# An encoder block with 32 experts: each partition takes four adjacent weight rows, in a ring of ten slots of 2 MB

## The chip, the cores and the metric

The kernel runs on one core of one Trainium2 chip. The metric is the device time of one execution in microseconds. Before the change the median of three runs is 1483.31 us (1477.65 to 1484.72).

## What is computed

One layer of a streaming encoder on 256 tokens of width 1024, in float32: a mixer of stick-breaking attention and a state-space scan, cross-attention into 256 memory tokens, and a mixture of 32 experts of which each token takes four. Only the last part is touched:

```python
def expert(xt, e):            # xt: the rows of tokens that chose expert e
    g = min(xt @ w_e_gate[e] + b_e_gate[e], 7.0)
    u = clip(xt @ w_e_up[e] + b_e_up[e], -7.0, 7.0)
    return (g * sigmoid(1.702 * g) * (u + 1)) @ w_e_down[e] + b_e_down[e]
h = layer_norm(alpha * h + sum(weight[t, e] * expert(h[t], e) for the 4 experts of t))
```

Each of the three matrices of an expert is 1024 x 1024 float32, 4 MB; all 96 are read, 384 MB.

## The kernel before

Up to about 530 us the mixer and the attentions run; their weights (`W`) come through SP's DMA queue, are split by ScalarE and VectorE into two parts (L96, L97) and multiplied on TensorE (L241 to L244). From then on the experts run, in 8 quads of four, each quad in two pairs.

*Weights.* An expert's matrix is fetched in chunks (`fetch`, `slot`), in the order gate and up of one expert, gate and up of its neighbour, down of both. A chunk is 256 rows of 1024 numbers, 1 MB: partition p takes the two adjacent rows 2p and 2p + 1, 8 KB in one run. The ring has 21 slots of 8 KB per partition, in four pools (`MR = 7, 7, 3, 4`) that open as space comes free. SP issues a fetch into a slot once the matmuls that read it are done. While the attention runs, each load of its weights lets one fetch of the first pool follow (`W.beside`).

*Matmuls.* `matmul_cols` (L950) multiplies a chunk: for each of the two rows k and each half i of the 1024 columns one matmul of 64 slots (tokens) by 512 columns. The 64 tokens of an expert are gathered from the normalised rows by a one-hot matrix (`gather`, L979): the rows x are the operand that is loaded into the array, 128 of their columns at a time. As partition p of a chunk holds rows 2p and 2p + 1, the columns are taken at every second place: `pairs(kt)` is `slice(256 * (kt // 2) + kt % 2, 256 * (kt // 2) + 256, 2)`. The gathered block xg gets the gain and bias of the norm (`gb2`, laid out in the same way). Gate and up (with a bias matmul L904 first, by `bias`) go to PSUM banks; `swiglu` (VectorE L955, L957 to L959, ScalarE L956) makes `ut`; `act_t` (L967) transposes it with four matmuls, again with columns at every second place; the down matmuls (`ps_y`, L950) follow, and `scatter` (L1000 to L1002) adds the result to the rows.

There are 32 gather matmuls per quad (8 column tiles, two parts of x, two token blocks) and four transposes per expert.

*Order.* A recording layer sets the order on each engine from the operations and its own costs, mixing pieces of neighbouring experts; a bias matmul for the next expert needs a PSUM bank whose previous tenant VectorE has read. SP, TensorE, VectorE and ScalarE each take their rows in that order.

*Further blocks.* If an expert has more than 64 tokens, a loop under a branch (`overflow`, L1083) runs the rest after quad 3, with weights in slots of the ring that the surrounding fetches leave free (four slots). With these inputs the loop has no turn, but each engine passes the branch. The last expert's w_down is fetched in smaller pieces (256 KB, in column quarters) for a finer end.

Of the kernel before, what the change touches and what calls it, by code (L numbers as in the profile page):

```python
# [39 lines left out]
MR = 7, 7, 3, 4  # L40
# [78 lines left out]
def body(nc, tc, a, out, dbg=None, stop=99):  # L119
# [7 lines left out]
    with es:  # L127
# [505 lines left out]
        if stop <= 2:  # L633
# [8 lines left out]
                for c in range(4)]  # L642
# [3 lines left out]
        def slot():  # L646
            turn[0] += 1
            return ring[(turn[0] - 1) % nslots].tile([P, 2, D], F32, tag="mw", name="mw")

        def fetch(upto):  # L650

            if not looped[0]:
                upto = min(upto, len(plan) // 2 + nslots - 4)
            while len(got) < min(upto, len(plan)):
                w, e, c = plan[len(got)]
                t = slot()
                if w == 2 and e == NE - 1:

                    t = t.rearrange("p j (k i f) -> p (j k) i f", k=2, i=2)
                    v = wes[w][e].rearrange("(c g p k) (j i f) -> c g p k j i f", c=2, g=2, p=P, j=2,  # L660
                                            i=2)[c % 2, :, :, :, :, c // 2]
                    for g in range(2):
                        for i in range(2):
                            nc.sync.dma_start(t[:, 2 * g:2 * g + 2, i], v[g, :, :, i])
# [61 lines left out]
        rows2 = xt_p.tile([8, 256], F32, name="rows2")  # L726
        for j, n in enumerate(("ln2_g", "ln2_b")):
            nc.sync.dma_start(rows2[4 * j:4 * j + 4], a[n][0].rearrange("(c f) -> c f", f=256))
# [4 lines left out]
        nc.vector.tensor_copy(gb2, ps[:, :16].rearrange("p (k j) -> p k j", k=2))  # L733
# [212 lines left out]
        def matmul_cols(dst, lhs, chunk, c, first=False):  # L946

            for k in range(2):
                for i in range(2):
                    nc.tensor.matmul(dst[i], lhs(2 * c + k), chunk[:, k, 512 * i:512 * i + 512],  # L950
                                     start=first and c == 0 and k == 0, stop=c == 3 and k == 1,
                                     skip_group_check=True)
# [8 lines left out]
        def pairs(kt):  # L961

            return slice(256 * (kt // 2) + kt % 2, 256 * (kt // 2) + 256, 2)

        def act_t(ut, pa, aT):
            for f in range(4):
                nc.tensor.transpose(pa[:, P * f:P * f + P], ut[:, pairs(f)], ident)  # L967
            nc.scalar.activation(aT, pa.rearrange("p (f i c) -> p f i c", f=4, i=2), AF.Copy)  # L968

        def gather(sel, xg, n, ps, kts=(0, KT)):  # L970

            w = 512 // n
            for kt in range(*kts, w):
                p = ps()
                for i in range(w):
                    o = p[:, n * i:n * i + n]
                    for x in (xh, xl):
                        for b in range(NB):
                            nc.tensor.matmul(o, x[:, b, pairs(kt + i)], sel[:, b], start=i == 0 and b == 0 and x is xh,  # L979
                                             stop=b == NB - 1 and x is xl, skip_group_check=True)  # L980
                for i in range(w):
                    o, g, b_ = p[:, n * i:n * i + n], *[gb2[:, (kt + i) % 2, 4 * j + (kt + i) // 2:4 * j + (kt + i) // 2 + 1]
# [74 lines left out]
        def overflow():  # L1057

            nv = nc.values_load(nov[0:1, 0:1], min_val=0, max_val=15)
            wb = [slot() for _ in range(3)]  # L1060
            ys = slot().rearrange("p k (h f) -> p (k h) f", h=2)
            ys = [ys[:, k].bitcast(F32R) for k in range(4)]
# [20 lines left out]
            with tc.If(nv > 0), tc.For_i(0, nv, 1):  # L1083
# [27 lines left out]
                n = 0  # L1111
                dst = [[pg[0][0:64], pg[0][64:128]], [pg[1][0:64], pg[1][64:128]], [y2[0][0:64], y2[1][64:128]]]
                for w in range(3):
# [3 lines left out]
                    for c in range(4):  # L1117
                        wt = wb[n % 3]
                        n += 1
                        nc.sync.dma_start(wt, wes[w][bass.ds(ev, 1), 256 * c:256 * c + 256].rearrange(  # L1120
                            "o (p k) f -> p (o k) f", p=P))
# [239 lines left out]
```

## Time and profile before

| | |
|---|---|
| median of 3 runs | 1483.31 us |
| profiled execution, its own time | 1483.58 us |
| its span | 1481.9 us |
| TensorE busy | 1391.4 us, 94% |
| DMA | 489.69 MB, mean 330 GB/s |
| mean granted TensorE clock | 0.985 |

The page lists what each engine did in one profiled execution. PE is TensorE's matmuls, PEld its weight loads, which overlap with them; DVE is VectorE, ACT ScalarE, SP the engine that issues the DMAs (SPq its queue). A duration of a matmul in a row of its own is longer than the distance between two of them, since they overlap; the distance is read from a run: its length over its number. A wait is idle time of an engine, with what ended it.

### The profile page before, as it was taken

What the parts mean: (1) busy time and instruction counts of PE and PEld (TensorE: products, weight loads), DVE (VectorE), ACT (ScalarE), POOL (GpSimd) and SP (SyncE); (2) the same over time, 40 slices, a digit from 0 to 9 for tenths busy, and PEclk for the clock granted to TensorE, in tenths of its full rate; (3) what the DMA queues carried; (4) which work ended last, traced back from release to release, by engine and by line L of the source; (5) the groups of instructions that cost most, each with busy time, mean ns of one, the idle gap of its engine ahead of it and who ended that gap; (6) DMA issues with size and microseconds to landing.
All of it is one profiled execution on the core that took longest, in us unless ns stands there. A gap on an engine that the chain in (4) does not pass through costs nothing. (4 is left out here: it accounts for less than half of the span.)

```text
span 1481.9 us, 19128 instructions
## 1 busy us (share of the span) xinstructions
PE 1391.4 (94%) x7888; PEld 802.9 (54%) x7888; DVE 635.1 (43%) x1004; ACT 416.4 (28%) x656; POOL 16.8 (1%) x36
## 2 busy tenths in 40 slices
PE   7999998998999999999999999979999999998996
PEld 7989898997999853333333333324334333323332
DVE  7766568998886551532222121222212212222213
ACT  5575678886555410010010000001001001001010
POOL 1000000000000010000000000000000000000001
PEclk9999999999999999999999999999999999999998
DMA  7545345543685789999999999999999999999995
GB/s 244 171 163 179 124 162 171 199 153 132 254 298 177 284 316 421 420 393 413 418 420 420 419 420 420 419 419 373 419 419 420 420 419 420 419 419 419 420 420 202
DMA packets 103503, 489.69 MB, mean 330 GB/s; under 512 B 10422, under 2 KB 15030, under 8 KB 54774
## 3 DMA queue, kind: packets, MB, share of 16 engines
q1 hardware_dynamic: 103140, 488.17, 83.2%
q8 instruction: 63, 1.03, 0.3%
q10 hardware_dynamic: 274, 0.27, 0.1%
q14 instruction: 26, 0.21, 0.0%
HBM read 487.33 MB, written 1.08 MB: 330 GB/s over the span
## 5 line engine op out<-in xcount | busy, mean ns | idle before, releaser
L950 PE MATMUL ps_gu<-mw,xg 128*64 128x512 f32 x2048 | 464.0, 595 | 1.0 <-DMA mw<-in_w_e_up 1.0
L950 PEld LDWEIGHTS ps_gu<-mw,xg 128*64 128x64 f32 x2048 | 146.5, 137 | 271.3 <-issue 256.5
L950 PE MATMUL ps_y<-mw,aT 128*64 128x512 f32 x992 | 225.4, 597 | 1.7 <-DMA mw<-in_w_e_down 1.6
L97 DVE TENSOR_TENSOR w_l<-w_raw,w_h 128x1024 fp32r<-128x1024 f32 x145 | 175.3, 1215 | 87.4 <-ACT w_h L96 85.5
L96 ACT ACTIVATE w_h<-w_raw 128x1024 fp32r<-128x1024 f32 x145 | 152.8, 1056 | 117.2 <-PE ps_t L243 73.0
L241 PE MATMUL ps_t<-hTh,w_h 128*128 128x256 f32 x576 | 164.0, 286 | 2.0 <-DVE gx L331 2.0
L243 PE MATMUL ps_t<-hTl,w_h 128*128 128x256 f32 x576 | 164.1, 285 | 0.0
L244 PE MATMUL ps_t<-hTh,w_l 128*128 128x256 f32 x576 | 162.7, 284 | 0.3 <-DVE w_l L97 0.3
L950 PEld LDWEIGHTS ps_y<-mw,aT 128*64 128x64 f32 x992 | 71.8, 138 | 137.5 <-issue 130.6
L241 PEld LDWEIGHTS ps_t<-hTh,w_h 128*128 128x128 f32 x576 | 110.0, 191 | 3.3 <-issue 3.1
L957 DVE TENSOR_SCALAR ut<-ps_gu 128x512 f32<-128x512 f32 x32 | 22.1, 691 | 206.3 <-PE ps_gu L950 206.1
L243 PEld LDWEIGHTS ps_t<-hTl,w_h 128*128 128x128 f32 x576 | 110.1, 191 | 0.2 <-issue 0.2
L244 PEld LDWEIGHTS ps_t<-hTh,w_l 128*128 128x128 f32 x576 | 109.6, 191 | 0.5 <-DVE w_l L97 0.5
L968 ACT ACTIVATE aT<-ps_x 128x512 f32<-128x512 f32 x32 | 19.1, 597 | 314.0 <-PE ps_x L967 313.9
L904 PE MATMUL ps_gu<-bgu,ident 128*64 128x512 f32 x256 | 72.0, 630 | 28.9 <-DVE ut L957 13.5
L955 DVE TENSOR_SCALAR gt<-ps_gu 128x512 f32<-128x512 f32 x32 | 22.1, 690 | 158.4 <-PE ps_gu L950 158.4
L995 DVE SCALAR_TENSOR_TENSOR y<-ps_y,scl,y 128x512 fp32r<-128x512 f32 x30 | 22.5, 750 | 153.5 <-ACT y L994 147.7
L994 ACT ACTIVATE y<-ps_y,scl 128x512 fp32r<-128x512 f32 x30 | 19.0, 684 | 222.2 <-PE ps_y L950 177.7
L956 ACT ACTIVATE st<-gt 128x512 f32<-128x512 f32 x32 | 20.1, 629 | 198.2 <-DVE gt L955 198.2
L904 PEld LDWEIGHTS ps_gu<-bgu,ident 128*64 128x64 f32 x256 | 17.1, 141 | 73.2 <-DVE ut L957 29.5
L1002 DVE TENSOR_TENSOR h<-h,ps_x 128x512 f32<-128x512 f32 x60 | 38.7, 681 | 15.2 <-PE ps_x L1001 15.2
L987 ACT ACTIVATE xg<-ps_x,gb 128x256 f32<-128x256 f32 x32 | 18.1, 564 | 94.4 <-PE ps_x L979 94.4
(354 smaller groups left out, 1798.3 us busy)
## 6 DMA issues: line engine op xcount, KB each, us to landing
mw<-in_w_e_gate SPq DMA_DIRECT2D x128, 1024.0 KB, 19.9
mw<-in_w_e_up SPq DMA_DIRECT2D x128, 1024.0 KB, 10.2
mw<-in_w_e_down SPq DMA_DIRECT2D x124, 1024.0 KB, 19.9
w_raw<-in_w_in SPq DMA_DIRECT2D x39, 1024.0 KB, 5.4
w_raw<-in_w_ssd SPq DMA_DIRECT2D x8, 1024.0 KB, 5.0
w_raw<-in_w_sb SPq DMA_DIRECT2D x4, 1024.0 KB, 5.1
csb<-csd SPq DMA_DIRECT2D x8, 512.0 KB, 6.4
w_raw<-in_w_mix_out SPq DMA_DIRECT2D x4, 1024.0 KB, 5.1
```

The lines of the kernel that those rows point to most:

```text
L96: nc.scalar.activation(h, src, AF.Copy)
L97: nc.vector.tensor_tensor(l, src, h.bitcast(F32), op=ALU.subtract)
L241: nc.tensor.matmul(o, wh[:, k, s], xh[:, kt], start=first and j % 2 == 0, stop=False, skip_group_check=True)
L243: nc.tensor.matmul(o, wh[:, k, s], xl[:, kt], start=False, stop=False, skip_group_check=True)
L244: nc.tensor.matmul(o, wl[:, k, s], xh[:, kt], start=False, stop=last, skip_group_check=True)
L904: nc.tensor.matmul(pg[w][64 * i:64 * i + 64], hot4(2 * w + i), bgu, start=True, stop=False, skip_group_check=True)
L950: nc.tensor.matmul(dst[i], lhs(2 * c + k), chunk[:, k, 512 * i:512 * i + 512], start=first and c == 0 and k == 0, stop=c == 3 and k == 1, ...
L955: nc.vector.tensor_scalar(gt, pg[0], LIMIT, None, op0=ALU.min)
L956: nc.scalar.activation(st, gt, AF.Sigmoid, scale=1.702)
L957: nc.vector.tensor_scalar(ut, pg[1], -LIMIT, LIMIT, op0=ALU.max, op1=ALU.min)
L995: nc.vector.scalar_tensor_tensor(yl[r], y2[i][r], scl[r, i:i + 1], yh[r].bitcast(F32), op0=ALU.mult, op1=ALU.subtract)
L1002: nc.vector.tensor_tensor(h2[:, b, s], h2[:, b, s], ps, op=ALU.add)
```

## The change

A chunk becomes 512 rows, 2 MB: partition p takes the four adjacent rows 4p to 4p + 3, 16 KB in one run. The ring has ten slots of 16 KB per partition (`MR = 3, 3, 2, 2`). The columns of x and `ut` are therefore taken at every fourth place (`fours`), and gb2 is laid out to match, with four small transposes in place of two. Each chunk has eight matmuls. The loop for further blocks takes one slot and uses its halves in turn; its result's buffer (`o_ys`) and the last gains (`gb3`) have a pool of their own, `spare`. The last w_down is fetched in the same pieces of 256 KB, laid out for the new rows.

```diff
-MR = 7, 7, 3, 4
+MR = 3, 3, 2, 2
...
-                for c in range(4)]
+                for c in range(2)]
...
-            return ring[(turn[0] - 1) % nslots].tile([P, 2, D], F32, tag="mw", name="mw")
+            return ring[(turn[0] - 1) % nslots].tile([P, 4, D], F32, tag="mw", name="mw")
...
-                upto = min(upto, len(plan) // 2 + nslots - 4)
+                upto = min(upto, len(plan) // 2 + nslots - 1)
...
-                ins = nc.sync.dma_start(t, wes[w][e, 256 * c:256 * c + 256].rearrange("(p k) f -> p k f", p=P))
+                ins = nc.sync.dma_start(t, wes[w][e, 512 * c:512 * c + 512].rearrange("(p k) f -> p k f", p=P))
...
-        gb2 = cst.tile([P, 2, 8], F32, name="gb2")
+        gb2 = cst.tile([P, 4, 4], F32, name="gb2")
...
-        for k in range(2):
-            nc.tensor.transpose(ps[:, 8 * k:8 * k + 8], rows2[:, k:256:2], ident[:8, :8])
+        for k in range(4):
+            nc.tensor.transpose(ps[:, 4 * k:4 * k + 4], rows2[:, k:512:4], ident[:4, :4])
...
+        spare = es.enter_context(tc.tile_pool(name="spare", bufs=1, reuse_waits="tile"))
...
-            for k in range(2):
-                for i in range(2):
-                    nc.tensor.matmul(dst[i], lhs(2 * c + k), chunk[:, k, 512 * i:512 * i + 512],
+            for k in ks:
+                for i in range(2):
+                    nc.tensor.matmul(dst[i], lhs(4 * c + k), chunk[:, k, 512 * i:512 * i + 512],
...
-        def pairs(kt):
-            return slice(256 * (kt // 2) + kt % 2, 256 * (kt // 2) + 256, 2)
+        def fours(kt):
+            return slice(512 * (kt // 4) + kt % 4, 512 * (kt // 4) + 512, 4)
...
-                nc.tensor.transpose(pa[:, P * f:P * f + P], ut[:, pairs(f)], ident)
+                nc.tensor.transpose(pa[:, P * f:P * f + P], ut[:, fours(f)], ident)
...
-                            nc.tensor.matmul(o, x[:, b, pairs(kt + i)], sel[:, b], start=i == 0 and b == 0 and x is xh,
+                            nc.tensor.matmul(o, x[:, b, fours(kt + i)], sel[:, b], start=i == 0 and b == 0 and x is xh,
...
-            wb = [slot() for _ in range(3)]
-            ys = slot().rearrange("p k (h f) -> p (k h) f", h=2)
+            wb = slot()
+            ys = spare.tile([P, 4, 512], F32R, tag="spare", name="o_ys")
```

The added line moves the lines behind it by one: L950, L967, L979 and L1083 of before are L951, L968, L980 and L1084 after.

The order on TensorE is laid out anew. First, on TensorE in the second pair of a quad, where the up matmuls of an expert end (ps_gu_6769 before, ps_gu_6672 after), with the bias matmuls of the next tenant of that bank (ps_gu_7045 and ps_gu_6924) and the down matmuls (ps_y). Before:

```order
L950 MATMUL ps_gu_6769<-mw,xg 64x512 x16
L904 MATMUL ps_gu_7045<-bgu,ident 64x512 x2
L950 MATMUL ps_y_6690<-mw,aT 64x512
L950 MATMUL ps_y_6691<-mw,aT 64x512
L950 MATMUL ps_y_6690<-mw,aT 64x512
L950 MATMUL ps_y_6691<-mw,aT 64x512
L967 MATMUL ps_x<-ident,ut 128x128 x4
```

And after, at the same place:

```order
L951 MATMUL ps_gu_6672<-mw,xg 64x512 x16
L951 MATMUL ps_y_6601<-mw,aT 64x512
L951 MATMUL ps_y_6602<-mw,aT 64x512
L951 MATMUL ps_y_6601<-mw,aT 64x512
L951 MATMUL ps_y_6602<-mw,aT 64x512
L951 MATMUL ps_y_6601<-mw,aT 64x512
L951 MATMUL ps_y_6602<-mw,aT 64x512
L951 MATMUL ps_y_6601<-mw,aT 64x512
L951 MATMUL ps_y_6602<-mw,aT 64x512
L904 MATMUL ps_gu_6924<-bgu,ident 64x512 x2
L968 MATMUL ps_x<-ident,ut 128x128 x4
```

The two bias matmuls stood right behind the last matmul of the bank's previous tenant; now a chunk of eight down matmuls stands between.

Second, on SP around the branch of the loop (the loop's own DMAs left out, which stand between the two pieces of each). Before:

```order
L668 DMA mw<-in_w_e_down 128x2048
L1083 COMPARE_AND_BRANCH x2
...
L1083 UNCONDITIONAL_BRANCH x2
L668 DMA mw<-in_w_e_down 128x2048 x3
L668 DMA mw<-in_w_e_up 128x2048
```

And after:

```order
L668 DMA mw<-in_w_e_down 128x4096
L1084 COMPARE_AND_BRANCH x2
...
L1084 UNCONDITIONAL_BRANCH x2
L668 DMA mw<-in_w_e_gate 128x4096
L668 DMA mw<-in_w_e_down 128x4096 x3
L668 DMA mw<-in_w_e_gate 128x4096 x2
```

Before, the first fetches behind the branch finish the down matrix whose first chunk stands ahead of it; after, one gate chunk comes first.

## Rows read from the trace of the kernel before

**Rows 1.** The page's first two parts: the span; busy time, share and number of instructions of each engine; and the span in 40 equal slices of 37 us (busy tenths of TensorE and its granted clock; the DMA engines' share in tenths; GB/s), with the number of DMA packets and their bytes below.
```profile
span 1481.9 us, 19128 instructions
...
PE 1391.4 (94%) x7888; PEld 802.9 (54%) x7888; DVE 635.1 (43%) x1004; ACT 416.4 (28%) x656; POOL 16.8 (1%) x36
...
PE   7999998998999999999999999979999999998996
...
PEclk9999999999999999999999999999999999999998
DMA  7545345543685789999999999999999999999995
GB/s 244 171 163 179 124 162 171 199 153 132 254 298 177 284 316 421 420 393 413 418 420 420 419 420 420 419 419 373 419 419 420 420 419 420 419 419 419 420 420 202
DMA packets 103503, 489.69 MB, mean 330 GB/s; under 512 B 10422, under 2 KB 15030, under 8 KB 54774
```

**Rows 2.** Three windows of the expert stage: window and its length in us, busy time and instructions of each engine, granted clock, share of the DMA engines, GB/s.
```profile
core 0: us, PE busy (x) PEld busy (x) DVE busy (x) ACT busy (x) POOL busy (x), PEclk, DMA share, GB/s
...
640.00:1000.00 360.00, 333.82 (x1556) 124.45 (x1552) 83.27 (x144) 30.96 (x51) 0.00 (x0) 0.99 1.01 416
...
1061.00:1320.00 259.00, 244.54 (x1132) 90.65 (x1128) 60.06 (x103) 22.52 (x37) 0.00 (x0) 0.99 1.01 419
1320.00:1440.00 120.00, 109.87 (x522) 41.11 (x524) 26.74 (x46) 11.46 (x19) 0.00 (x0) 1.00 1.01 420
```

**Rows 3.** TensorE's waits: which matmul (tile and line) waited for which instruction; us in total, times, the longest. First between 640 and 1000 us, then the two for weights between 1061 and 1482 us.
```profile
PE ps_gu L904 <- DVE ut L957: 6.3, 8, 0.8
PE ps_x L1000 <- ACT y L994: 4.7, 6, 0.8
PE ps_gu L904 <- DVE gt L955: 4.0, 5, 0.8
PE ps_x L1000 <- DVE h L1002: 3.4, 4, 0.8
PE ps_x L967 <- DVE ut L959: 1.2, 2, 0.6
PE ps_x L979 <- DVE h L1002: 0.5, 2, 0.3
...
PE ps_y L950 <- DMA mw<-in_w_e_down: 1.6, 3, 0.6
PE ps_gu L950 <- DMA mw<-in_w_e_up: 1.0, 3, 0.6
```

**Rows 4.** The chain of waits between 1000 and 1062 us, in order of time: start, duration, engine, tile, line, and how many instructions in a run.
```profile
1006.69 2.12 PE ps_x L979 x16
...
1009.83 1.17 PE ps_x L979 x8
...
1028.82 1.72 PE ps_gu L950 x8
1030.53 0.68 PE ps_x L967 x4
```

**Rows 5.** Four lines by themselves (L967, L979, L858, L241): weight loads (PEld) or matmuls (PE), their number, shortest, median and longest duration in ns, first and last start, and shapes.
```profile
L967 PEld LDWEIGHTS ps_x<-ident,ut x128: 194/209/219, 562.9 to 1448.9; 128*128 128x128 f32 x128
L967 PE MATMUL ps_x<-ident,ut x128: 281/283/386, 562.9 to 1449.0; 128*128 128x128 f32 x128
...
L979 PEld LDWEIGHTS ps_x<-sel,xh x128: 192/198/333, 535.1 to 1356.0; 128*128 128x128 f32 x128
L979 PE MATMUL ps_x<-sel,xh x128: 280/284/583, 535.1 to 1356.1; 128*128 128x256 f32 x128
L979 PEld LDWEIGHTS ps_x<-sel,xl x128: 193/198/331, 535.5 to 1356.2; 128*128 128x128 f32 x128
...
L858 PE MATMUL ps_l<-wr,x2T x32: 192/276/297, 522.9 to 529.7; 128*128 128x32 f32 x32
...
L241 PEld LDWEIGHTS ps_t<-hTh,w_h x576: 186/188/337, 13.2 to 376.9; 128*128 128x128 f32 x192
```

**Rows 6.** TensorE's timeline around 528 us: start, duration of the run, line, output and operands, shapes, number.
```profile
528.02 1.97 PE L858 MATMUL ps_l<-wr,x2T 128*128 128x32 f32 x16 [0.25 <-ACT x2T L855]
```

**Rows 7.** Windows ahead of the expert stage, columns as in rows 2.
```profile
20.00:30.00 10.00, 10.00 (x88) 10.00 (x87) 5.26 (x8) 5.74 (x9) 0.00 (x0) 1.00 0.75 219
100.00:200.00 100.00, 100.00 (x733) 89.53 (x733) 62.82 (x78) 67.43 (x102) 0.00 (x0) 1.00 0.48 159
...
300.00:400.00 100.00, 94.06 (x748) 87.81 (x747) 86.76 (x113) 68.88 (x111) 1.56 (x5) 0.97 0.50 179
```

**Rows 8.** TensorE's waits for VectorE at the bias matmuls over the whole span, columns as in rows 3.
```profile
PE ps_gu L904 <- DVE ut L957: 13.5, 17, 0.8
...
PE ps_gu L904 <- DVE gt L955: 9.4, 12, 0.8
```

**Rows 9.** The longest wait of SP's queue (SPq), columns as in rows 3.
```profile
SPq L82 <- DVE w_l L97: 333.2, 58, 12.5
```

**Rows 10.** TensorE's timeline behind the branch; in brackets the idle time ahead and what ended it (PEq is TensorE's sequencer).
```profile
1000.21 6.48 PE L904 MATMUL ps_gu<-bgu,ident 128*64 128x512 f32 x16 [6.00 <-PEq L1083]
```

**Rows 11.** Two windows of 20 us behind the branch, columns as in rows 2.
```profile
1000.00:1020.00 20.00, 19.79 (x88) 8.71 (x89) 4.50 (x12) 2.26 (x4) 0.00 (x0) 0.85 0.90 372
1020.00:1040.00 20.00, 20.00 (x96) 8.08 (x95) 3.46 (x5) 1.86 (x3) 0.00 (x0) 1.00 0.93 378
```

More of the change, by code (lines that the diff above doesn't have):

```diff
@@ L945, in body, with matmul_cols @@
         ring += [p for p, n in zip((mr2, mr3, mr4), MR[1:]) for _ in range(n)]
-        def matmul_cols(dst, lhs, chunk, c, first=False):
-            for k in range(2):
+        def matmul_cols(dst, lhs, chunk, c, first=False, ks=range(4)):
+            for k in ks:
                 for i in range(2):
-                    nc.tensor.matmul(dst[i], lhs(2 * c + k), chunk[:, k, 512 * i:512 * i + 512],
-                                     start=first and c == 0 and k == 0, stop=c == 3 and k == 1,
+                    nc.tensor.matmul(dst[i], lhs(4 * c + k), chunk[:, k, 512 * i:512 * i + 512],
+                                     start=first and c == 0 and k == 0, stop=c == 1 and k == 3,
                                      skip_group_check=True)
@@ L1059, in overflow @@
             nv = nc.values_load(nov[0:1, 0:1], min_val=0, max_val=15)
-            wb = [slot() for _ in range(3)]
-            ys = slot().rearrange("p k (h f) -> p (k h) f", h=2)
-            ys = [ys[:, k].bitcast(F32R) for k in range(4)]
+            wb = slot()
+            ys = spare.tile([P, 4, 512], F32R, tag="spare", name="o_ys")
+            ys = [ys[:, k] for k in range(4)]
             sel = mt.tile([P, NB, 4, CAP], F32R, tag="sel", name="o_sel")
@@ L1116, in overflow @@
                         act_t(ut, pa, aT)
[L1117 to L1121, printed above, removed]
-                        lhs = (lambda kt: aT[:, kt % 4, kt // 4]) if w == 2 else (lambda kt: xg[:, kt, 0:CAP])
-                        matmul_cols(dst[w], lhs, wt, c, first=w == 2)
+                    for c in range(2):
+                        for k in (0, 2):
+                            wt = wb[:, k:k + 2]
+                            nc.sync.dma_start(wt, wes[w][bass.ds(ev, 1), 512 * c:512 * c + 512].rearrange(
+                                "o (p k) f -> p (o k) f", p=P)[:, k:k + 2])
+                            lhs = (lambda kt: aT[:, kt % 4, kt // 4]) if w == 2 else (lambda kt: xg[:, kt, 0:CAP])
+                            matmul_cols(dst[w], lhs, wb, c, first=w == 2, ks=(k, k + 1))
                 scatter(y2, scl, selT, [slice(0, 64), slice(64, 128)], lambda: pa, lambda i: ys[2 * i:2 * i + 2])
@@ L1143, in last_rows @@
         def last_rows():
-            gb = slot()
+            gb = spare.tile([P, 2, D], F32, tag="spare", name="gb3")
             for j, n in enumerate(("ln3_g", "ln3_b")):
@@ L1199, in body, with project @@
                     pg = pg0 if e == 0 else bank_pair()
-                    def project(w, c):
+                    def project(w, c, ks=range(4)):
                         i = turn_of[w, e, c]
@@ L1215, in body @@
                         fill(2, 4)
-                        for c in range(4):
-                            project(0, c)
-                            if c < 2:
-                                fill(2 * c + 4, 2 * c + 6)
+                        for c in range(2):
+                            for k in (0, 2):
+                                project(0, c, (k, k + 1))
+                                if c == 0:
+                                    fill(k + 4, k + 6)
                         for i in range(2):
@@ L1225, in body @@
                         pair_weights()
-                        for c in range(4):
+                        for c in range(2):
                             project(1, c)
@@ L1234, in body @@
                     for w in range(2) if e > 0 else ():
-                        for c in range(4):
+                        for c in range(2):
                             project(w, c)
@@ L1248, in body @@
                         break
-                    for c in range(4):
+                    for c in range(2):
                         i = turn_of[2, e0 + 2 * pr + q, c]
@@ L1252, in body @@
                         matmul_cols(dst, lambda kt: aT[:, kt % 4, kt // 4], got[i], c, first=True)
-                        if e == NE - 1 and c == 1:
+                        if e == NE - 1 and c == 0:
                             acc.append(start_acc(1))
@@ L1273, in second @@
                 for i in range(2):
[L1274 removed]
+                    nc.tensor.matmul(dst[i][:, s], aT[:, kt % 4, kt // 4], got[-2 + c // 2][:, kt, i],
                                      start=c + k == 0, stop=kt == KT - 1, skip_group_check=True)
```

24 lines of the change are left out of this document (11 added, 13 removed).

## The prediction

> **What bounds the kernel now.** I read the page first: the span, the busy shares and the forty slices [rows 1]. TensorE is busy 94% of 1481.9 us, no other engine half of it; from slice 15 on (some 550 us) the DMA engines are full too, at about 420 GB/s. Two resources are thus near their limit in the expert stage, and the averages don't say which one paces it. So I read the expert stage in windows [rows 2]: between 640 and 1000 us TensorE is busy 333.8 of 360 us, between 1061 and 1320 us 244.5 of 259, with a DMA share of 1.01 in both. Then I asked what ends the rest of TensorE's time there [rows 3]: in the first of these windows only VectorE and ScalarE (the PSUM bank of the previous expert not yet read, 0.8 us each time), and no transfer at all; after 1061 us weights are waited for six times, 1.6 + 1.0 = 2.6 us in all. TensorE sets the pace, and the transfers, full as they are, are just ahead of it. What counts is therefore what the change adds to or takes from TensorE's row of instructions; a quicker transfer is worth at most those 2.6 us.
>
> The next view is the chain of waits through expert work [rows 4]: it goes along TensorE nearly throughout, so an added time there is added to the end, one to one. It also gives the pace of each kind of matmul. An expert matmul (L950, 512 columns) takes 1.72 / 8 = 0.215 us. The gather matmuls (L979) take 2.12 us in a run of 16 and 1.17 us in a run of 8, so one more costs (2.12 - 1.17) / 8 = 0.119 us; four transposes (L967) take 0.68 us. The operand that these two lines load into the array (`x[:, b, pairs(kt)]`, `ut[:, pairs(f)]`) is read at every second number; all else is read in a row.
>
> **The change part by part.**
> *Bytes, matmuls, VectorE, ScalarE.* The same 12 MB per expert and the same 48 matmuls of it; no engine gets other work. Two more transposes of four columns for gb2: under 1 us, in the time before the experts, left out.
>
> *The loads at a step of four.* `fours` doubles the step in L979 and L967 from 8 to 16 bytes. They are 256 + 128 = 384 loads of 128 columns [rows 5]. What sets their pace is the load, not the matmul: 128 moving columns (L967) and 256 (L979) both go at about 0.12 us, and a matmul with only 32 moving columns but a load in a row (L858) takes 1.97 us for 16 [rows 6], with the last one's 0.28 us (its median in rows 5) off (1.97 - 0.28) / 15 = 0.113 us. Loads in a row with 256 moving columns go at 10 us / 88 = 0.114 us [rows 7]. So a step of two numbers has cost 0.119 - 0.113 = 0.006 us per load. Nothing in the trace reads at a step of four. Bounds: it may gain, if the 0.006 was an accident of the neighbours, 384 x -0.006 = -2.3 us; it may stay at 0.119, 0 us; it may add 0.006 again for each further step, 384 x 0.012 = +4.6 us; and it may double with the span that it reads, to 0.238, 384 x 0.119 = +45.7 us. The small rise from one to two reads best to me as the point where reading has just become slower than the array: below it the step is free, above it the time grows with the span. A load that falls behind then takes about two of those in a row, 0.22 us; I take +0.10 us, 384 x 0.10 = **+38.4 us**, the rows nearest to it being those of the loads in a row, taken twice. All of it lies on the path, since such a load starts with its matmul and nothing else of TensorE runs beside a run of them.
>
> [...] The rows show 0.113 us for a load in a row and 0.119 us at a step of 8 bytes [rows 4, 6]. [...] No run so far shows a step of four.
>
> *The order on TensorE.* A chunk is now eight matmuls (3.44 us) where it was four (1.72 us), and the order on TensorE was laid out anew. Two bias matmuls (L904) stood right behind the last matmul of the bank's previous tenant before; in some places a chunk of `y` stands between them now (the first piece of order shown with the change). Each such place costs a wait of 13.5 / 17 = 0.79 us for VectorE [rows 8]. By the order I count 30 places before and 25 after, so -5 x 0.79 = **-4.0 us**. In three quads the four plus four matmuls of a scatter have become two plus six; each can add a wait for VectorE or ScalarE of 0.8 us [rows 3], two of them taken: **+1.7 us**. Bounds: -8 us (ten places gone) to +3 us.
>
> *The ring.* Ten slots of 2 MB hold 20 MB, where 21 held 21. Up to the branch of the loop SP may have fetched 105 x 2 = 210 MB, before 192 + 17 = 209 MB: equal. A slot comes free, and a chunk can be used, in steps of 2 MB: at 420 GB/s 5.0 us in place of 2.5. As long as TensorE paces, this is hidden behind a ring that holds some 50 us of work. If TensorE gets slower by 38 us, the transfers are further ahead at the end than now, and the DMA waits of [rows 3] go: **-2.6 us**. If it doesn't get slower, TensorE catches up with them as now, and then waits for whole 2 MB: 0 to +5 us, which belongs to the rivals.
>
> *Longer packets.* Each partition's run grows from 8 to 16 KB. Between 100 and 400 us, with runs of 2 KB, 159 GB/s at a share of 0.48 make 331 GB/s for full engines, 179 at 0.50 make 358 [rows 7]; runs of 8 KB make 416 / 1.01 = 412 [rows 2]. The gain of a doubling thus falls off; for the next one I take 0 to 5%. TensorE's pace makes it worth nothing beyond the 2.6 us already counted.
>
> *Early fetches beside the attention weights.* Three of 2 MB in place of seven of 1 MB: 6 MB instead of 7. One weight load more or less beside them costs TensorE nothing there, since its loads wait for VectorE and not for the queue (SP's L82 waits, 333.2 us [rows 9]); priced at 0, at worst one wait of the length of a 2 MB transfer, +5 us.
>
> *The branch.* TensorE stops once for 6.0 us there [rows 10]; SP has to see its transfers land, which are as many bytes as before, and the first chunk issued behind it is another (a gate one, second piece of order). The one slot that the loop has now, in place of four, is refilled from there. The DMA share is 0.90 and 0.93 around it [rows 11]; 0 us, at worst +3 us for code that is fetched anew.
>
> Sum: the profiled execution's own time is 1483.58 us (1481.9 us of span and 1.7 us around it), 0.3 us above the median of the three runs. 1483.6 + 38.4 - 4.0 + 1.7 - 2.6 = **1517 us**.
>
> **The rivals.**
> *The step of four is free* (ends on the other side, faster). Then 1483.6 - 4.0 + 1.7 - 2.6 = 1478.7 us if the longer packets bring weights sooner, and 1476 us with no scatter waits added. For it: a step of two costs 0.006 us only, and the loads of [rows 5] differ little in length between a row (188 ns at L241) and a step of two (198 ns at L979). Against it: that there is a difference at all. It decides from an added cost under some 8 ns per load on (384 x 8 ns = 3 us); up to there the shorter waits prevail.
> *A small further step, or the coarse ring takes back the waits.* +0.006 to +0.04 us per load makes +2 to +15 us; or the loads are free and TensorE, 5 us earlier, runs into transfers which at a share of 1.01 have nothing to give, and waits for whole 2 MB: 1483.6 - 4.0 + 1.7 + (0 to 5), 1481 to 1486 us. For it: DMA waits have begun after 1061 us [rows 3]. Middle: 1486 us.
> *The transfers don't get longer packets*, because a packet is cut at some size: nothing would change in the sum, as the packets pay for nothing there; the count of packets would show it.
>
> **How the numbers follow.** Forecast 0.63, its own range 1500 to 1526 us (loads at +0.06 to +0.12 us, 23 to 46 us, with the order's bounds). Free loads 0.21, 1472 to 1481 us. The small step or the coarse ring 0.16, 1481 to 1496 us. A difference within 0.5%, 1475.9 to 1490.7 us, is about what a measurement of this kernel can't tell from none. Of the free loads I count half as faster by more than that and half as the same; of the third case two thirds as the same and one third as slower; with 0.03 moved from slower to faster for savings that I don't see: faster 0.14, same 0.21, slower 0.65. The range has to reach to the free loads: 1476 to 1524 us leaves about one in ten out on either side.
>
> **What would show it.** In the timeline and the chain of the kernel after, the runs of L980 and L968: a run of 16 of 2.12 us becomes about 3.6, a run of eight 1.17 about 1.9, four transposes 0.68 about 1.05. TensorE's busy time in a stretch of expert work stays above 90%, DMA share falls to about 0.97 and GB/s to about 400, and TensorE's waits for weights go from 2.6 us to none. The waits of L904 fall by about five. Packets under 8 KB stay, those of 8 KB and more halve from 103,503 - 54,774 = 48,729 [rows 1]. The forecast is wrong if those runs last as long as now (then the time is below 1481 us), or if the waits for weights grow by over 5 us.

## The result, and the profile after

The kernel after takes 1497.23 us (median of 4 runs, 1495.65 to 1499.83) beside 1483.82 us for the kernel before on the same chip: ratio 1.0101, 95% interval 1.0070 to 1.0132. It is slower, by 13.4 us between the medians, where the forecast said 33.5 us (1517 us). The profiled execution has a span of 1496.1 us.

The page of the kernel after first: span, busy times, the rate of the transfers in 40 slices, the number of packets (answering to [rows 1]).

```profile
span 1496.1 us, 18742 instructions
...
PE 1413.6 (94%) x7890; PEld 830.1 (55%) x7890; DVE 635.6 (42%) x1004; ACT 416.2 (28%) x656; POOL 16.8 (1%) x36
...
GB/s 243 170 169 169 141 141 184 184 170 144 327 206 141 267 348 428 428 332 402 427 427 427 426 427 426 427 426 373 427 426 427 427 426 427 427 426 427 427 399 48
DMA packets 76133, 489.65 MB, mean 327 GB/s; under 512 B 7379, under 2 KB 11979, under 8 KB 51727
```

TensorE is busy 22.2 us longer (1391.4 before), the others as before. The transfers run at 427 GB/s in the expert stage where they ran at 420, and in the last two slices they are mostly done: they are further ahead of TensorE than before. Packets of 8 KB and more have halved, 76,133 - 51,727 = 24,406 for 48,729.

Next the chain of waits of the kernel after, between 1000 and 1062 us (columns as in [rows 4]), and under it two lines by themselves (as [rows 5]).

```profile
1013.66 3.94 PE ps_x L980 x16
...
1018.60 2.08 PE ps_x L980 x8
...
1041.13 0.68 PE ps_x L968 x4
```

```profile
L968 PEld LDWEIGHTS ps_x<-ident,ut x128: 195/212/231, 564.8 to 1463.7; 128*128 128x128 f32 x128
...
L980 PEld LDWEIGHTS ps_x<-sel,xh x128: 307/330/336, 534.8 to 1369.9; 128*128 128x128 f32 x128
```

The gather's run of 16 went from 2.12 to 3.94 us and its run of 8 from 1.17 to 2.08: one more matmul costs (3.94 - 2.08) / 8 = 0.233 us in place of 0.119. The four transposes, whose loads read at the same step of 16 bytes, still take 0.68 us. That is the first half of the answer, and it is plain in the loads too: 330 ns for 198 at the gather, 212 for 209 at the transposes.

TensorE's waits in the kernel after (as [rows 8] and the scatter's rows), and two windows (as [rows 2]):

```profile
PE ps_x L1001 <- ACT y L995: 10.9, 14, 0.8
PE ps_gu L904 <- DVE gt L956: 9.4, 12, 0.8
PE ps_x L1001 <- DVE h L1003: 9.0, 11, 1.1
PE ps_gu L904 <- DVE ut L958: 8.7, 11, 0.8
```

```profile
640.00:1000.00 360.00, 343.85 (x1560) 135.36 (x1556) 81.20 (x141) 30.96 (x51) 0.00 (x0) 0.99 0.98 414
...
1061.00:1320.00 259.00, 245.03 (x1116) 94.54 (x1114) 58.66 (x104) 21.18 (x35) 0.00 (x0) 0.99 1.01 427
```

No wait for an expert's weights is left among TensorE's waits. The bias matmuls wait 23 times where they waited 29.

Last, the page's sum of the chain of waits that ended last, which reaches back to 1000 us, as a share of the span. In the kernel before, with the step that follows on the stretch in [rows 4]:

```profile
DMA 20%; PE 11%; DVE 1%; issue 0%; ACT 0%; DVEq 0%; SPq 0%
```

```profile
1061.65 20.05 DMA mw<-in_w_e_up
```

And in the kernel after:

```profile
PE 30%; DVE 2%; ACT 0%; issue 0%; DVEq 0%
```

The prediction read this chain between 1000 and 1062 us, where it lies on TensorE. Behind that, in the kernel before, it lies on the transfers of weights until 1342.60 us, and once more from 1402.52 to 1422.40 us. So for most of this time the transfers ended last, with TensorE close beside them. In the kernel after, the transfers are not on it at all.

### The profile page after: what moved, and what is told of

It is laid out like the page before. It is cut to its first block, busy times and chain, and to the rows that moved or that the text cites. A ratio compares the mean times of both kernels' runs of the same rounds, so it can differ in the third digit from the quotient of the medians.

```text
span 1496.1 us, 18742 instructions
## 1 busy us (share of the span) xinstructions
PE 1413.6 (94%) x7890; PEld 830.1 (55%) x7890; DVE 635.6 (42%) x1004; ACT 416.2 (28%) x656; POOL 16.8 (1%) x36
## 2 busy tenths in 40 slices
DMA packets 76133, 489.65 MB, mean 327 GB/s; under 512 B 7379, under 2 KB 11979, under 8 KB 51727
## 5 line engine op out<-in xcount | busy, mean ns | idle before, releaser
L951 PE MATMUL ps_gu<-mw,xg 128*64 128x512 f32 x2048 | 462.0, 595 | 0.0
L951 PEld LDWEIGHTS ps_gu<-mw,xg 128*64 128x64 f32 x2048 | 147.4, 137 | 269.0 <-issue 262.4
L951 PE MATMUL ps_y<-mw,aT 128*64 128x512 f32 x992 | 222.2, 595 | 0.0
L241 PE MATMUL ps_t<-hTh,w_h 128*128 128x256 f32 x576 | 164.0, 286 | 2.0 <-DVE gx L331 2.0
L951 PEld LDWEIGHTS ps_y<-mw,aT 128*64 128x64 f32 x992 | 71.3, 138 | 134.0 <-issue 133.4
L241 PEld LDWEIGHTS ps_t<-hTh,w_h 128*128 128x128 f32 x576 | 109.9, 191 | 3.3 <-issue 3.1
L904 PEld LDWEIGHTS ps_gu<-bgu,ident 128*64 128x64 f32 x256 | 17.7, 140 | 66.4 <-issue 26.2
L988 ACT ACTIVATE xg<-ps_x,gb 128x256 f32<-128x256 f32 x32 | 18.1, 564 | 119.4 <-PE ps_x L980 119.4
## 6 DMA issues: line engine op xcount, KB each, us to landing
mw<-in_w_e_gate SPq DMA_DIRECT2D x64, 2048.0 KB, 18.1
```

Source lines behind the costliest of these rows:

```text
L241: nc.tensor.matmul(o, wh[:, k, s], xh[:, kt], start=first and j % 2 == 0, stop=False, skip_group_check=True)
L904: nc.tensor.matmul(pg[w][64 * i:64 * i + 64], hot4(2 * w + i), bgu, start=True, stop=False, skip_group_check=True)
L951: nc.tensor.matmul(dst[i], lhs(4 * c + k), chunk[:, k, 512 * i:512 * i + 512], start=first and c == 0 and k == 0, stop=c == 1 and k == 3, ...
```

## The experiments

All times below stand beside the kernel before on the same chip in the same job (medians 1482.87 to 1484.46 us). Experiments 4, 6 and 7 ran once each (1486.91, 1669.12 and 1506.75 us); of them only rows are read, not the time. In the edits, `...` marks code that is left out.

**1. The gather's step alone, in the kernel before** (e1_gather_step4).

```diff
-    nc.tensor.matmul(o, x[:, b, pairs(kt + i)], sel[:, b], ...
+    nc.tensor.matmul(o, x[:, b, 512 * ((kt + i) // 4) + (kt + i) % 4:512 * ((kt + i) // 4) + 512:4], sel[:, b], ...
```

> The kernel before with one line changed: the gather matmuls load x at every fourth column (other columns than the weights' rows, so the result differs), the order on every engine is the same as before. Theory (the gather's loads alone make the change slower): a run of eight goes from 1.17 to 2.08 us, 256 x 0.113 = +29 us, less up to 4 us of waits for weights that vanish: 1509 us (1505 to 1514). Rival 1 (the coarse ring or the order makes it slower): 1484 us, within 3.

Measured: 1501.29 us, ratio 1.0113 (1.0096 to 1.0130), +17.0 us. The chain of this kernel between 1000 and 1062 us shows the mechanism as expected:

```profile
1020.90 2.07 PE ps_x L979 x8
```

The step of the gather alone makes the kernel slower, with the old ring and the old order; the ring isn't needed for it. But 17 us is less than the 29 that 256 loads of +0.113 us would put on TensorE, and 1501 us lies below the 1505 to 1514 expected. The two profiled executions, 1498.0 - 1481.9 = 16.1 us apart, show where the rest is. The gather's two groups of matmuls, before (busy us, mean ns, idle time ahead):

```profile
L979 PE MATMUL ps_x<-sel,xh 128*128 128x256 f32 x128 | 30.9, 326 | 0.7 <-DVE h L1002 0.7
L979 PE MATMUL ps_x<-sel,xl 128*128 128x256 f32 x128 | 27.2, 297 | 0.0
```

And with the step of four:

```profile
L979 PE MATMUL ps_x<-sel,xh 128*128 128x256 f32 x128 | 43.5, 425 | 0.7 <-DVE h L1002 0.7
L979 PE MATMUL ps_x<-sel,xl 128*128 128x256 f32 x128 | 40.8, 404 | 0.0
```

They grow from 58.1 to 84.3 us, by 26.2 and not by 29. In the kernel before, the gathers of quads 0, 3, 5 and 6 ran partly at the lower clock (granted clock 0.72 from 535 to 541 us, 0.85 from 885 to 890, 0.84 from 1117 to 1122 and 0.88 from 1230 to 1235; 1.00 in windows over the other four), and so were already longer than 0.119 us a load (0.213 us at the start of quad 0); a load at a step of four is no longer at the lower clock than at the higher (3.94 and 3.95 us for 16, last section). The expert matmuls (L950) are busy 689.4 us before and 686.3 here. In all TensorE is busy 1411.4 - 1391.4 = 20.0 us longer and idle 90.5 - 86.6 = 3.9 us less, 2.6 of them the waits for weights: 20.0 - 3.9 = 16.1 us. Why the matmuls other than the gather's take some 6 us less, I can't say. Experiments 8 to 10 ask how much room the transfers have.

**2. The transposes' step alone, in the kernel before** (e2_transposes_step4).

```diff
-    nc.tensor.transpose(pa[:, P * f:P * f + P], ut[:, pairs(f)], ident)
+    nc.tensor.transpose(pa[:, P * f:P * f + P], ut[:, f:512:4], ident)
```

> The kernel before with one line changed: the four transposes of each expert load ut at every fourth column (result differs), order the same. Theory: nothing, 1484 us within 3, and four transposes still take 0.68 us. Rival 2 (every load of 128 numbers at 16 bytes pays, as forecast, and the trace of after hides it beside other work): four transposes at about 1.05 us, +12 us, 1496 us.

Measured: 1483.45 us beside 1484.33, ratio 0.9995 (0.9985 to 1.0005); the chain has "x4" in the same 0.68 us:

```profile
1029.77 0.68 PE ps_x L967 x4
```

The 128 loads of the transposes pay nothing. Rival 2 falls, and with it a third of the forecast's largest term (12.8 of 38.4 us).

**3. The kernel after without the gather's step** (e3_after_gather_step2).

```diff
-    nc.tensor.matmul(o, x[:, b, fours(kt + i)], sel[:, b], ...
+    nc.tensor.matmul(o, x[:, b, 256 * ((kt + i) // 2) + (kt + i) % 2:256 * ((kt + i) // 2) + 256:2], sel[:, b], ...
```

> The kernel after with one line changed: the gather matmuls load x at every second column as before (result differs), order and ring as in after. Theory: 1497 - 29 = 1468 us, up to 5 more if waits for weights come back: 1467 to 1474, which is faster than before by about 12 us, from shorter waits for VectorE, transfers of 427 in place of 420 GB/s, and fewer changes between kinds of matmul. Rival 1: 1490 us or more.

Measured: 1479.16 us, ratio 0.9978 (0.9964 to 0.9992). So the gather's step costs 18 us here, and the rest of the change is a small gain; rival 1 falls. Yet 1468 was expected. TensorE is busy 1413.6 - 1388.2 = 25.4 us less than in the kernel after, not 29, and idle 88.9 - 82.5 = 6.4 us more. Its waits and one window of this kernel say where the idle time comes from:

```profile
PE ps_y L951 <- DMA mw<-in_w_e_down: 7.1, 5, 3.4
```

```profile
1061.00:1320.00 259.00, 239.93 (x1118) 87.82 (x1116) 58.47 (x101) 21.13 (x35) 0.00 (x0) 0.99 1.01 426
```

As soon as TensorE is quicker, it waits for weights, up to 3.4 us at a time, at a DMA share of 1.01. The transfers then share the pace: on its page the chain that ended last lies for 13% of the span on them and for 17% on TensorE.

**4. What a load costs by its step** (e4_steps). The step changes from quad to quad; `stepped` takes it from `GS` (gather), and a like one for the transposes from `TS`.

```diff
+        GS, TS = (4, 1, 2, 3, 4, 6, 8, 5), (4, 1, 2, 3, 4, 4, 4, 4)
...
-                            nc.tensor.matmul(o, x[:, b, fours(kt + i)], sel[:, b], ...
+                            nc.tensor.matmul(o, x[:, b, stepped(kt + i)], sel[:, b], ...
```

> A measurement, on the kernel after: the gather's step in numbers of 4 bytes is 4, 1, 2, 3, 4, 6, 8, 5 in quads 0 to 7, the transposes' step 4, 1, 2, 3, then 4 (result differs). [...] By the span read: 0.119, 0.17, 0.232, 0.29, 0.35, 0.46 at 2, 3, 4, 5, 6, 8. Transposes: 0.11 to 0.12 us at every step by the theory, above 0.2 at step 4 by rival 2.

TensorE's timeline of this kernel in quads 1, 2 and 3 (steps 1, 2, 3); each row is two matmuls, so two starts with the rows between them give the distance:

```profile
660.18 0.40 PE L994 MATMUL ps_x<-sel,xl 128*128 128x256 f32 x2
...
661.13 0.40 PE L994 MATMUL ps_x<-sel,xl 128*128 128x256 f32 x2
...
770.26 0.41 PE L994 MATMUL ps_x<-sel,xl 128*128 128x256 f32 x2
...
771.73 0.40 PE L994 MATMUL ps_x<-sel,xl 128*128 128x256 f32 x2
...
882.28 0.51 PE L994 MATMUL ps_x<-sel,xl 128*128 128x256 f32 x2
...
884.37 0.51 PE L994 MATMUL ps_x<-sel,xl 128*128 128x256 f32 x2
```

The first two rows are 8 matmuls apart, 0.95 / 8 = 0.119 us; the next two 12, 1.47 / 12 = 0.122; the last two 12, 2.09 / 12 = 0.174. The chain in quads 4, 5, 6 and 7 (steps 4, 6, 8, 5) has the runs of eight:

```profile
1007.78 2.07 PE ps_x L994 x8
...
1123.90 2.03 PE ps_x L994 x8
...
1237.78 2.13 PE ps_x L994 x8
...
1353.96 2.02 PE ps_x L994 x8
```

So a matmul's load costs 0.12, 0.12, 0.17 and 0.23 us at steps of 4, 8, 12 and 16 bytes, and then about the same (2.02 to 2.13 us for eight at 20, 24 and 32 bytes, 2.07 at 16). The span that it reads doesn't set the price, since from 16 to 32 bytes the span doubles and the price stays. What fits is an estimate by the pieces of 16 bytes on which the 128 numbers lie: 64, 96 and 128 at steps of two, three and four or more. With 0.233 us / 128 = 1.8 ns for each (0.233 us from the chain of the kernel after) the first two come to 0.12 and 0.17 us, as measured (in a row, with 32 pieces, 0.119 us stay, so something else sets that). The runs show the prices; what in the memory or the array makes them is not shown. The transposes don't follow this estimate (0.68 us for four at steps of 8 and of 16 bytes; experiments 2 and 7). That a step of four float32 numbers is free, as the first rival has it, is refuted for a matmul's load and holds for a transpose's.

**5. Sorted columns** (e5_permuted_x). The split that writes x puts the columns in the order in which the gather reads them.

```diff
-    split(nc, xh[:, b, s], xl[:, b, s], h2[:, b, s], copy=copy, sub=nc.gpsimd)
+    split(nc, *[x[:, b, s].rearrange("p (k c) -> p k c", k=4) for x in (xh, xl)],
+          h2[:, b, s].rearrange("p (c k) -> p k c", k=4), copy=copy, sub=nc.gpsimd)
...
-    nc.tensor.matmul(o, x[:, b, fours(kt + i)], sel[:, b], ...
+    nc.tensor.matmul(o, x[:, b, P * (kt + i):P * (kt + i) + P], sel[:, b], ...
```

> The kernel after with two lines changed: the split of the normalised rows writes x with its columns already sorted by their place in four, so the gather loads 128 numbers in a row (the result is the reference's); order and ring as in after. Theory (TensorE gets back 26 us + 256 x 0.006 = 1.5 us more, and then the transfers set the end as in the run with a step of two): 1478 us (1474 to 1481), faster than before by 0.2 to 0.7%; gather runs of eight about 1.12 us; TensorE waits for down weights some 8 us in all. Rival (TensorE still paces): 1470 us. Rival (the reordering read of VectorE, ScalarE and GpSimd costs ahead of the first gather): 1484 or more.

Measured: 1478.87 us (12 runs) beside 1483.38, ratio 0.9972 (0.9961 to 0.9983): faster than both kernels, by 0.3% and by 1.2%. It is the change with the gather's cost taken out. The chain, and the wait for weights that remains:

```profile
1002.53 1.11 PE ps_x L980 x8
```

```profile
PE ps_y L951 <- DMA mw<-in_w_e_down: 5.2, 3, 3.4
```

**6. Why transposes don't pay: kind and width** (e6_kinds).

```diff
+        KIND = ((4, 256, 0), (1, 64, 1), (2, 64, 1), (4, 64, 1), (4, 128, 0), (1, 128, 0), (8, 64, 1), (4, 256, 0))
...
```

(step, moving columns, and 1 for plain float32, in quads 0 to 7.)

> A measurement on the kernel after, of why transposes don't pay: the gather in quads 1, 2, 3 and 6 as plain float32 matmuls of 64 moving columns (four for 256) with the stationary operand at a step of 1, 2, 4 and 8 numbers; in quads 4 and 5 as float32r with 128 moving columns at a step of 4 and 1; quads 0 and 7 as in after. [...] Theory B (the moving columns of 256 numbers and the load get in each other's way): float32r at step 4 with 128 moving columns falls to about 0.12 us. Theory C (only float32r pays): plain float32 stays at 0.12 us at every step.

A plain float32 matmul has two records here, each with its own load. The timeline in quads 1, 3 and 6 (plain, steps 1, 4 and 8) and in quad 4 (float32r, step 4, 128 moving columns):

```profile
661.32 2.00 PE L991 MATMUL ps_x<-sel,xh 128*128 128x64 f32 x16 [0.25 <-DVE h L1015]
...
956.34 3.99 PE L991 MATMUL ps_x<-sel,xh 128*128 128x64 f32 x16 [0.24 <-DVE h L1015]
...
1363.96 4.08 PE L991 MATMUL ps_x<-sel,xh 128*128 128x64 f32 x16 [0.24 <-DVE h L1015]
...
1129.05 1.09 PE L991 MATMUL ps_x<-sel,xl 128*128 128x128 f32 x4
1129.99 1.09 PE L991 MATMUL ps_x<-sel,xh 128*128 128x128 f32 x4
```

Plain float32 loads at steps 4 and 8 take twice the time of those in a row (3.99 and 4.08 us for 2.00), so theory C falls; with 128 moving columns a float32r load at step 4 still takes (1129.99 - 1129.05) / 4 = 0.235 us, so theory B falls. A matmul's load at 16 bytes thus costs about 0.23 us with 128 and with 256 moving columns, and double as plain float32 too; why a transpose's doesn't is not shown. Quad 2 ran at half the clock (0.50, last section), so it says nothing of step 2 at the full one; experiment 7 does (2.10 us for 16).

**7. The transpose or the operand** (e8_transpose_or_operand).

```diff
+        KINDS = ((0, 4), (1, 4), (1, 1), (1, 2), (2, 8), (2, 4), (2, 1), (2, 2))
...
```

(0: transposes of ut, 1: plain matmuls of ut with the identity, 2: transposes of x; and the step.)

> A measurement on the kernel after, of the four loads per expert behind swiglu: in quads 1, 2 and 3 plain float32 matmuls with the identity (64 moving columns, two for 128) in place of the transposes, with ut at a step of 4, 1 and 2 numbers; in quads 4 to 7 transposes of the first token block of x (a part of the gather's operand, in place of ut) at a step of 8, 4, 1 and 2. Theory (it is the transpose, not the operand): plain loads of ut at step 4 take 0.23 us, at 1 and 2 0.11 to 0.12; transposes of x stay at 0.11 to 0.12 us at every step, step 8 too. Rival (it is where or how ut is stored): plain loads of ut stay at 0.12 us, and transposes of x at steps 4 and 8 take 0.23 us.

The timeline of quads 1, 2 and 3 (plain matmuls of ut at steps 4, 1 and 2), then 4, 5 and 6 (transposes of x at steps 8, 4 and 1):

```profile
687.61 3.95 PE L977 MATMUL ps_x<-ident,ut 128*128 128x64 f32 x16
...
815.72 2.00 PE L977 MATMUL ps_x<-ident,ut 128*128 128x64 f32 x16
...
937.55 2.10 PE L977 MATMUL ps_x<-ident,ut 128*128 128x64 f32 x16
...
1102.24 1.17 PE L975 MATMUL ps_x<-ident,xh 128*128 128x128 f32 x8
...
1162.91 0.75 PE L975 MATMUL ps_x<-ident,xh 128*128 128x128 f32 x4
...
1274.37 0.66 PE L975 MATMUL ps_x<-ident,xh 128*128 128x128 f32 x4
```

The same ut at the same step costs double when it is loaded for a matmul (3.95 us for 2.00), and the gather's own x costs next to nothing more when it is loaded for a transpose: four in 0.75 us at a step of 16 bytes for 0.66 in a row, and eight in 1.17 us even at 32 bytes. It is the kind of instruction. Why a transpose's load is spared, no run shows.

**8. Is TensorE the only limit of the kernel before?** (e10_short_bias).

```diff
-    nc.tensor.matmul(pg[w][64 * i:64 * i + 64], hot4(2 * w + i), bgu, ...
+    nc.tensor.matmul(pg[w][64 * i:64 * i + 64, 0:128], hot4(2 * w + i), bgu[:, 0:128], ...
```

> The kernel before with the bias matmuls cut from 512 to 128 columns (the bias of the other columns of gate and up is left out); the order on SP and VectorE is the same, on TensorE nearly. It takes some 256 x 0.12 = 30 us from TensorE's row alone. If TensorE sets the pace of the kernel before, as the prediction said: 1455 us (1450 to 1460). If the transfers are as much a limit (which would explain that 26 us more on TensorE in the first run cost 17 us only): 1472 to 1480 us, with TensorE's waits for weights grown from 2.6 to 20 us or more.

Measured: 1480.51 us beside 1484.46, ratio 0.9976 (0.9966 to 0.9986): 28.1 us less of busy TensorE (1391.4 - 1363.3) give 4 us. That is just above the 1472 to 1480 us of the second case, and far from the first. Its waits for weights are 17.1 + 4.9 + 1.3 = 23.3 us, from 2.6:

```profile
PE ps_y L950 <- DMA mw<-in_w_e_down: 17.1, 26, 3.0
...
PE ps_gu L950 <- DMA mw<-in_w_e_up: 4.9, 8, 2.0
...
PE ps_gu L950 <- DMA mw<-in_w_e_gate: 1.3, 3, 0.5
```

In the kernel before, transfers and TensorE end nearly together, as its chain says too (20% of the span on the transfers). That the waits for weights were only 2.6 us showed how closely TensorE follows the transfers, not that these have room: nearly all that is taken from TensorE comes back as a wait for weights.

**9. Runs of 8 KB in the ring of 2 MB, with the quick gather** (e12_runs_of_8k, on the kernel of experiment 3) **and with the slow one** (e13_after_runs_of_8k, on the kernel after). The same edit in both:

```diff
-    nc.sync.dma_start(t, wes[w][e, 512 * c:512 * c + 512].rearrange("(p k) f -> p k f", p=P))
+    nc.sync.dma_start(t.rearrange("p (h k) f -> p h k f", h=2),
+                      wes[w][e, 512 * c:512 * c + 512].rearrange("(h p k) f -> p h k f", h=2, p=P))
```

> The third run's kernel (after, gather at a step of two) with one line changed: each 2 MB transfer brings two runs of 8 KB to a partition in place of one of 16 KB (result differs); slots, early fetches and the order on TensorE, VectorE and ScalarE are the same. Theory (with the gather out of the way the transfers set the end, and the longer run is what makes them quicker): 420 in place of 427 GB/s, TensorE's waits for weights grow from 7 us, and the time from 1479 to 1484 to 1491 us. Rival (the length of the run doesn't matter, TensorE or the ring sets the end): 1479 us, within 3.

> The kernel after with one line changed: each 2 MB transfer brings two runs of 8 KB to a partition in place of one of 16 KB (result differs); the gather stays at a step of four, the order on TensorE, VectorE and ScalarE is the same. Theory (with the slow gather TensorE sets the end, and the transfers have room): 1497 to 1502 us, so that the longer run, worth 12 us with a quick gather, is worth 0 to 5 here. Rival (the longer run is worth its 12 us in either case): 1509 us.

Measured: 1491.09 us (ratio 1.0051, 1.0035 to 1.0067) with the quick gather, 12 us above experiment 3; 1497.15 us (1.0104, 1.0087 to 1.0121) with the slow one, the same as after. The quick one's waits for weights and its window:

```profile
PE ps_y L951 <- DMA mw<-in_w_e_down: 11.5, 9, 3.6
```

```profile
1061.00:1320.00 259.00, 237.46 (x1096) 87.66 (x1098) 59.34 (x102) 20.98 (x35) 0.00 (x0) 0.99 1.01 420
```

| time in us | gather at step 2 | gather at step 4 |
|---|---|---|
| runs of 8 KB, ring of 2 MB slots | 1491.1 | 1497.2 |
| runs of 16 KB, ring of 2 MB slots | 1479.2 | 1497.2 |

The longer run is worth some 12 us with the quick gather, where TensorE waits for the transfers, and nothing where TensorE alone sets the end; the gather's step is worth 18 us in one row and 6 in the other. With runs of 8 KB and the old step, the new ring and order are 8.2 us slower than the kernel before: this is what the coarse slots, the smaller early fetch and the new order cost together when the transfers share the pace. How it divides wasn't tried, but the traces give a hint: up to 640 us the kernel before moves 231 GB/s, and experiments 9 and 10 move 228, so they are 3 GB/s x 640 us = 1.9 MB behind by then. At 420 GB/s that is an estimated 4.6 us, over half of the 8.2, and points to the smaller early fetch.

**10. Two transfers per slot** (e7_two_dmas), on the kernel of experiment 3.

```diff
-                ins = nc.sync.dma_start(t, wes[w][e, 512 * c:512 * c + 512].rearrange("(p k) f -> p k f", p=P))
-                if len(ring) < nslots:
+                src, ks = wes[w][e, 512 * c:512 * c + 512].rearrange("(p k) f -> p k f", p=P), ((0, 4),) if len(ring) < nslots else ((0, 2), (2, 4))
+                for ins in [nc.sync.dma_start(t[:, k0:k1], src[:, k0:k1]) for k0, k1 in ks][:len(ring) < nslots]:
```

> The kernel after with the gather at a step of two (result differs, as in the third run) and each 2 MB slot filled by two transfers of two rows per partition, 8 KB in one run, once the ring is whole; the order on TensorE then goes in steps of four matmuls again, as before. Theory (the rest of the change is faster by longer transfers and by an order with fewer waits): both are gone, 1484 us (1480 to 1488), 420 GB/s. Rival (the coarse landing of 2 MB is what TensorE waits for in the third run): faster than the third run's 1479 us, 1473 to 1477.

Measured: 1488.21 us, ratio 1.0034 (1.0021 to 1.0047), just above the 1480 to 1488 us that the theory gave. It lands in steps of 1 MB and still waits for weights:

```profile
PE ps_y L951 <- DMA mw<-in_w_e_down: 6.1, 7, 2.8
```

The rival (the coarse landing alone) falls, but as run length and order change together here, the run says little more than experiment 9.

## Why the prediction was wrong

*The loads at a step of four, +38.4 us for 384 loads.* This is the step that failed: it priced the 128 loads of the transposes like the 256 of the gather. For the transposes 12.8 us were taken, and they cost 0 (experiments 2 and 7). For the gather 25.6 us were taken, and its matmuls are busy 84.4 us for 58.1, 26.3 more: right in kind and in size. That the size fits is partly luck: a load takes 0.113 us more and not 0.10, and the stretches at the lower clock in the kernel before bring 29 down to 26 (experiment 1). I had put the two lines together because both had the same pace at a step of two, 0.12 us; but a common pace at one step doesn't show a common cause, and the kind of the instruction was never weighed. The bounds given (0 to 45.7 us) held both. The reason given, time that grows with the span that is read, is wrong too: beyond 16 bytes it doesn't grow (0.23 to 0.24 us at steps of 16 to 32 bytes, experiment 4).

*TensorE sets the pace, and its added time goes to the end one to one.* The premise was misread. The chain "goes along TensorE nearly throughout" only in the 62 us that were shown; over the whole span the page has 20% of it on the transfers and 11% on TensorE. The two end nearly together, so the two directions differ. Time taken from TensorE turns into waits for weights (experiment 8: 28 us less busy, 4 us gained). Time added to it arrives nearly whole: in experiment 1, 20.0 us more busy became 16.1, less the 2.6 us of waits for weights, which the forecast had counted, and 1.3 us of others. For this change, which adds, the misreading cost little; for the 1468 us expected in experiment 3, which takes away, it cost 6 of the 11 us missed.

*A quicker transfer is worth at most 2.6 us.* Right for the kernel after (experiment 9: 0), wrong as a statement on the parts: with the gather's cost taken out it is worth 12 us. Run length (-12 us) and ring, early fetches and order together (+8 us) work against each other, and the slow gather hides both.

*The order, -4.0 + 1.7 us.* The waits of the bias matmuls fell from 13.5 + 9.4 = 22.9 us to 18.1, by 4.8 us and six waits (five were counted); those of the scatter rose from 10.1 + 7.7 = 17.8 us over the whole span ([rows 3] show one window of them) to 19.9, by 2.1. Net -2.7 us for -2.3. Experiment 1 beside the kernel after, both with a slow gather, differ by 4.1 us in their medians, but their intervals overlap.

*The waits for weights, -2.6 us.* Gone, as forecast.

*The branch and the early fetches, 0 us.* Not tried by themselves. The kernel after is behind by 3 GB/s up to 640 us as well (228 for 231), but TensorE doesn't wait for it.

Two slips in the working change nothing in the forecast: the first rival without scatter waits is 1483.6 - 4.0 - 2.6 = 1477 us, not 1476; and 0.215 us is the pace of one record of an expert matmul, which leaves two (0.43 us together, as the 3.44 us for a chunk of eight have it).

Taken together, forecast and the two profiled executions of [rows 1] and the page of after:

| part, in us | forecast | measured |
|---|---|---|
| transposes (busy 23.8, then 24.3) | +12.8 | +0.5 |
| gather (58.1, then 84.4) | +25.6 | +26.3 |
| expert matmuls (689.4, then 684.2) | 0 | -5.2 |
| all other busy time of TensorE | 0 | +0.6 |
| idle time of TensorE (90.5, then 82.5) | -4.9 | -8.0 |
| sum | +33.5 | +14.2 |

Besides the transposes, the expert matmuls are the term that the forecast lacked. 3.1 of their 5.2 us are gone in experiment 1 too, which has the old order, so the order alone isn't the reason, and it stays open. The first rival (the step is free) was right for one of the two lines. Of the second (the coarse ring takes back what is saved) experiment 9 shows a cost of ring, early fetches and order together; in the kernel after it doesn't come to bear.

## What to carry to other kernels

When a layout for longer transfers changes the step at which another engine reads, price that step by kind of instruction, each with a run of its own: here a matmul's load at 16 bytes took double (0.233 us for 0.119) and a transpose's next to nothing more (0.68 us for four at 8 and at 16 bytes). The step could here be moved to the instruction that writes the operand, where it was hidden: sorting the columns at the split turned +13 us into -4.5. And small waits for a resource whose share is 1.01 don't mean that it has room: read the chain that ended last over the whole span, not in one stretch, and take 30 us from the engine that seems to pace to see what is left, before a removed time is carried to the end in full.

## What was not expected of the hardware

The cost of a matmul's load rises with the step only up to 16 bytes: 0.12, 0.12, 0.17, 0.23 us and then 0.23 to 0.24 at 20, 24 and 32 bytes (experiment 4), and transposes are all but spared (0.11 us in a row, 0.11 to 0.12 at steps of 8 to 32 bytes).

In experiment 6 the granted clock stood at half (0.50 to 0.54 in the windows below) through most of the gathers of quads 2, 3 and 6, whose loads stride and have 64 moving columns each, though TensorE shows no gap in them (25.00 of 25.00 us busy in quad 2); the gather of quad 1, of the same shape with loads in a row, ran at the full clock (1.00). In quad 2 the clock had fallen already in the scatter (its last matmuls take 0.63 us, in quad 1 0.40), behind waits of 0.78 and 0.85 us; in quads 3 and 6 it fell in the first 4 us of the gather, behind waits of 0.85 and 0.24 us. Quad 1 had waits of 0.85 and 0.25 us and no fall; why the clock falls is not shown. The windows of that kernel in quads 1, 2 and 3 (granted clock before the last two columns); quad 6 has 0.50 from 1366 to 1420 us:

```profile
662.00:675.00 13.00, 13.00 (x119) 13.00 (x118) 0.54 (x1) 0.56 (x1) 0.00 (x0) 1.00 0.34 141
795.00:820.00 25.00, 25.00 (x119) 25.00 (x119) 0.54 (x1) 0.56 (x1) 0.00 (x0) 0.50 0.74 313
957.00:985.00 28.00, 28.00 (x122) 28.00 (x121) 0.54 (x1) 0.56 (x1) 0.00 (x0) 0.54 0.64 269
```

What the lower clock cost a load depended on its step. The timeline of that kernel at the start of quad 2 (step 2, half the clock), and the second run of quad 3 (step 4, half the clock):

```profile
794.14 3.67 PE L991 MATMUL ps_x<-sel,xh 128*128 128x64 f32 x16
...
960.13 3.94 PE L991 MATMUL ps_x<-sel,xl 128*128 128x64 f32 x16
```

At a step of two 16 loads take 3.67 us there and 2.10 at the full clock (experiment 7); at a step of four they take 3.94 us there and 3.95 at the full clock. At that step the load went at the same pace at either level of the clock.

A run of 16 KB per partition gave 427 GB/s where one of 8 KB gave 420, at the same DMA share of 1.01: 1.7%, and some 12 us of 1480 in a kernel that waits for it.
